# Rows set aside for instruction fetches, one bound register for all indexed transfers, and a branch laid out the other way, in an argmax, gather and scatter kernel

## The chip, the cores and the metric

The kernel runs on one core of a Trainium2 chip. The time is the device time of one execution in microseconds (us), and medians of several executions are given. All runs told here are "fast" (granted clock 1.0). The profile's span, which starts and ends inside the execution, is 1.8 us shorter than the time.

## The reference

```python
def setup_inputs():
    B, S, H = (8, 2048, 2560)
    return {'scores': randn(B, S, S), 'values': randn(B, S, H)}      # float32, seeded

def reference(scores, values):
    best_j = np.argmax(scores, axis=2)                    # a row number for each row of scores
    gathered = values[b_idx, best_j, :].copy()
    out = np.zeros_like(values)
    np.add.at(out, (b_idx, best_j, slice(None)), gathered)
    return out
```

Row j of `out` is row j of `values` times the number of times that j was an argmax in its batch. With these inputs 6,131 of the 16,384 rows have the count 0, 5,875 the count 1 and 4,378 a count of 2 or more.

## The kernel before

VectorE finds the argmaxes, TensorE counts them, and GpSimd issues indirect transfers of 128 rows: single rows straight from `values` to `out`, repeated rows in through SBUF (scaled by ScalarE) and out again, zero rows from a row of zeros. A transfer's index list names a row of `out` or a number out of bounds. In the trace a row moved is a packet of 10,240 B and 385 ns; an entry out of bounds moves no row and leaves a 4 B packet of 9 ns (medians).

```python
def scatter_rows_in_dram(nc, out, in_, idx, bound): ...   # single rows; takes its bound from a register
last_row = nc.gpsimd.to_reg(B * S - 1)
...
ZCAP, MCAP = 7, 5
ZLAST = 12
CORR = 56
...
def scatter(v, idx, note=writes_out):                     # zero rows and repeated rows
    note(nc.gpsimd.indirect_dma_start(
        out=out_flat[:, :], out_offset=bass.IndirectOffsetOnAxis(ap=idx, axis=0),
        in_=v, in_offset=None, bounds_check=B * S - 1, oob_is_err=False))
```

A transfer of 128 rows is split over 16 DMA engines, 8 rows to each: with such shares one assignment fits all 44,928 data packets of the trace (the sorting is in the prediction). In the last batch the kernel evens the engines out: it counts for each engine the rows of all other work and hands out the 746 zero rows of that batch so that the sums agree, within a cap of `CORR` rows between engines.

```python
def level_engines(rank):
    ...   # copies: single rows by engine; load: zero rows of the other batches, repeated rows of all
    nc.vector.scalar_tensor_tensor(out=work[:], in0=load[:, 1, :], scalar=2.0, in1=load[:, 0, :], op0=ALU.mult, op1=ALU.add)
    nc.vector.tensor_tensor(out=work[:], in0=work[:], in1=copies[:], op=ALU.add)
    nc.vector.tensor_reduce(out=top[:], in_=work[:], op=ALU.max, axis=X)
    ...   # more = min(top - work, CORR); even = the rest divided by 16, rounded up
    nc.vector.tensor_scalar(out=quota[:], in0=more[:], scalar1=even[:, 0:1], scalar2=None, op0=ALU.add)
    ...   # the zero rows are dealt out in the order of the engines until they are used up
```

At the end comes code for inputs that overflow the kernel's fixed numbers of transfers. It isn't needed here, and a branch passes it by; then GpSimd waits for the last transfers.

```python
more = nc.values_load(over_i[0:1, 0:1], engines=[ET.Pool, ET.DVE, ET.PE], min_val=0, max_val=2)
with tc.If(more > 0):
    ...   # one transfer at a time, long
last = nc.gpsimd.wait_ge(landed, 16 * n_free[0])
```

Of the kernel before, what the change touches and what calls it, by code (L numbers as in the profile page):

```python
# [8 lines left out]
FP32 = mybir.dt.float32  # L9
# [4 lines left out]
ALU = mybir.AluOpType  # L14
P = 128
# [21 lines left out]
def kernel(  # L37
# [6 lines left out]
    nc = tc.nc  # L44
    B, S, S2 = scores.shape
# [11 lines left out]
    NE = 16  # L57
    LE = P // NE
    ZCAP, MCAP = 7, 5
    ZLAST = 12  # L60
    ZHEAD = 4
    CORR = 56

    values_flat = values.rearrange("b s h -> (b s) h")
    out_flat = out.rearrange("b s h -> (b s) h")
    last_row = nc.gpsimd.to_reg(B * S - 1)

    consts = ctx.enter_context(tc.tile_pool(name="consts", bufs=1))
# [41 lines left out]
    nc.vector.tensor_scalar(out=rowset[:], in0=lane_f[:, 0:NE], scalar1=part8_f[:, 0:1], scalar2=None, op0=ALU.is_equal)  # L110
    up_f = consts.tile([P, NE], FP32)
    nc.vector.tensor_scalar(out=up_f[:], in0=lane_f[:, 0:NE], scalar1=-1.0, scalar2=NE - 1.0, op0=ALU.mult, op1=ALU.add)
    tots = consts.tile([P, 2, B], FP32)
    most = consts.tile([P, 1], FP32)
    notone = consts.tile([P, NT], FP32)
# [22 lines left out]
    while x < B * NT:  # L138
        n = 1
# [12 lines left out]
    def writes_out(ins):  # L152

        tc.declare_no_dep(ins.ins, group="out", reason="disjoint rows")
        tc.add_to_no_dep_group("out", ins.ins)

    def after_waits(ins):
        tc.declare_no_dep(ins.ins, group="zrow", reason="GpSimd has waited for the transfers ahead of it")
# [12 lines left out]
    def gather(v, idx, note=lambda ins: None):  # L171
        note(nc.gpsimd.indirect_dma_start(  # L172
            out=v, out_offset=None, in_=values_flat[:, :],
            in_offset=bass.IndirectOffsetOnAxis(ap=idx, axis=0), bounds_check=B * S - 1, oob_is_err=False))

    def scatter(v, idx, note=writes_out):
        note(nc.gpsimd.indirect_dma_start(  # L177
            out=out_flat[:, :], out_offset=bass.IndirectOffsetOnAxis(ap=idx, axis=0),
            in_=v, in_offset=None, bounds_check=B * S - 1, oob_is_err=False))

    vslot = [0]
    tiles = [0]
# [6 lines left out]
    def find_maxima(rows, t, am):  # L189

        g = t % G
        if g == 0:
            am = small.tile([P, G, 8], U32, name="am")
        mx = small.tile([P, 8], FP32, name="mx")
        nc.vector.max(out=mx[:], in_=rows)  # L195
        nc.vector.max_index(out=am[:, g, :], in_max=mx[:], in_values=rows)  # L196
        return am
# [60 lines left out]
    def level_engines(rank):  # L258
# [12 lines left out]
            out=share[:], in0=tots[:].rearrange("p c b -> p (c b)").unsqueeze(1).to_broadcast([P, NE, 2 * B]),  # L271
            in1=up_f[:].unsqueeze(2).to_broadcast([P, NE, 2 * B]), op=ALU.add)
# [3 lines left out]
        nc.vector.tensor_reduce(out=load[:, 1, :], in_=share[:, :, B:2 * B], op=ALU.add, axis=X)  # L276
        work = lev.tile([P, NE], FP32)
        nc.vector.scalar_tensor_tensor(out=work[:], in0=load[:, 1, :], scalar=2.0, in1=load[:, 0, :], op0=ALU.mult, op1=ALU.add)
        nc.vector.tensor_tensor(out=work[:], in0=work[:], in1=copies[:], op=ALU.add)
        top = lev.tile([P, 1], FP32)  # L280
        nc.vector.tensor_reduce(out=top[:], in_=work[:], op=ALU.max, axis=X)
        more = lev.tile([P, NE], FP32)
# [3 lines left out]
        fits = lev.tile([P, 1], FP32)  # L286
        nc.vector.tensor_single_scalar(out=fits[:], in_=zeros, scalar=float(NE * (NT * LE - CORR)), op=ALU.is_le)
        nc.vector.tensor_scalar(out=more[:], in0=more[:], scalar1=float(CORR), scalar2=fits[:, 0:1], op0=ALU.min, op1=ALU.mult)
        all_more = lev.tile([P, 1], FP32)
# [14 lines left out]
            out=past[:], in0=rank.unsqueeze(2).to_broadcast([P, NT, NE]),  # L304
            in1=ends[:].unsqueeze(1).to_broadcast([P, NT, NE]), op=ALU.is_ge)
# [13 lines left out]
    def value_steps(b, cnt_ps):  # L319
# [43 lines left out]
        if b == B - 1:  # L363
            level_engines(rank[:, 0, :])
# [42 lines left out]
        def gathers():  # L407
            for k in range(MCAP):
                v = stage()
                gather(v, mi[:, k:k + 1])  # L410
                nc.scalar.activation(out=v, in_=v, func=mybir.ActivationFunctionType.Copy, bias=0.0,  # L411
                                     scale=mc[:, k:k + 1])
                staged.append(v)
                if rest:
                    copy_once(rest.pop(0))

        def zeros(columns):
            for k in columns:
                scatter(zrow[:], zi[:, k:k + 1], free_running)
                if rest:  # L420
                    copy_once(rest.pop(0))
# [3 lines left out]
        if b == 0:  # L425
            zeros(range(ZHEAD))

# [3 lines left out]
            yield  # L431
            zeros(range(ZHEAD, nz))
        else:
            gathers()
            zeros(range(ZHEAD))
        for k in range(MCAP):

            scatter(staged[k], mi[:, k:k + 1], writes_out if b * MCAP + k < B * MCAP - NV else free_running)
        if b > 0:
            zeros(range(ZHEAD, nz))  # L440
        assert not rest
# [39 lines left out]

    more = nc.values_load(over_i[0:1, 0:1], engines=[ET.Pool, ET.DVE, ET.PE], min_val=0, max_val=2)
    spilt = tc.alloc_semaphore("spilt")
    with tc.If(more > 0):

        n_spilt = 0
        last = nc.gpsimd.wait_ge(landed, 16 * n_free[0])

        def one_by_one(ins):
            nonlocal n_spilt, last  # L490
            writes_out(ins)
            after_waits(ins)
            tc.add_to_no_dep_group("zrow", ins.ins)
            ins.then_inc(spilt, 16)
            tc.info.no_tile_sem_insts.add(ins.ins.name)
            n_spilt += 1
            with tc.issue_after(ins.ins):
                last = nc.gpsimd.wait_ge(spilt, 16 * n_spilt)

        for b in range(B):  # L500
            for k in range(ZLAST if b == B - 1 else ZCAP, NT):
                with tc.issue_after(last.ins):
                    scatter(zrow[:], zero_i[:, b * NT + k:b * NT + k + 1], one_by_one)

        for b in range(B):
            for k in range(MCAP, NM):
                i = b * NM + k
                with tc.issue_after(last.ins):
                    gather(zrow[:], many_i[:, i:i + 1], one_by_one)
                with tc.issue_after(last.ins):  # L510
                    scaled = nc.gpsimd.tensor_scalar(
                        out=zrow[:], in0=zrow[:], scalar1=many_c[:, i:i + 1], scalar2=None, op0=ALU.mult)
                after_waits(scaled)
                with tc.issue_after(scaled.ins):
                    scatter(zrow[:], many_i[:, i:i + 1], one_by_one)

        for b in range(FAST):
            cnt_ps = psum_c.tile([P, NT], FP32)
            am = None
            for t in range(NT):  # L520
                rows = room[:, 0:S]
                with tc.issue_after(last.ins):
                    after_waits(nc.gpsimd.dma_start(out=rows, in_=scores[b, t * P:(t + 1) * P, :]))
                am = find_maxima(rows, t, am)
                if t % G == G - 1:
                    count_places(am, t, cnt_ps)
            cnt = fin.tile([P, NT], FP32)
            nc.vector.tensor_copy(cnt[:], cnt_ps[:])
            some_f = fin.tile([P, NT], FP32)
            nc.vector.tensor_scalar(out=some_f[:], in0=cnt[:], scalar1=0.0, scalar2=BIG, op0=ALU.is_equal, op1=ALU.mult)  # L530
            nc.vector.scalar_tensor_tensor(out=some_f[:], in0=some_f[:], scalar=float(b * S), in1=row_f[:], op0=ALU.add, op1=ALU.add)
            nc.vector.tensor_copy(some_i[:, b * NT:(b + 1) * NT], some_f[:])
            for t in range(NT):
                with tc.issue_after(last.ins):
                    empty = nc.gpsimd.memset(zrow[:], 0.0)
                after_waits(empty)
                with tc.issue_after(empty.ins):
                    gather(zrow[:], some_i[:, b * NT + t:b * NT + t + 1], one_by_one)
                with tc.issue_after(last.ins):
                    scaled = nc.gpsimd.tensor_scalar(out=zrow[:], in0=zrow[:], scalar1=cnt[:, t:t + 1], scalar2=None, op0=ALU.mult)  # L540
                after_waits(scaled)
                with tc.issue_after(scaled.ins):
                    one_by_one(nc.gpsimd.dma_start(out=out_flat[b * S + t * P:b * S + (t + 1) * P, :], in_=zrow[:]))
# [34 lines left out]
```

## Time and profile before

| | before |
|---|---|
| time, median of 6 | 826.94 us (826.55 to 827.45) |
| span of the profile | 825.1 us |
| DMA engines | 347.13 MB, mean 421 GB/s, full in 39 of 40 slices |
| VectorE, GpSimd busy | 73%, 33% |
| GpSimd's last transfer issued | 809.97 us |
| instruction fetches (queues 14 and 8) | 17 of 8192 B and 6 of 16,384 B |

The prediction reads the busy rows and the queues line by line. What it tells of windows is this view of the kernel before; columns are the window, its length, busy time and instructions of each engine, TensorE's clock, the mean busy share of the 16 DMA engines, and GB/s.

```profile
814.00:816.00 2.00, 0.00 (x0) 0.00 (x0) 0.00 (x0) 0.00 (x0) 0.00 (x0) 1.00 0.96 389
816.00:818.00 2.00, 0.00 (x0) 0.00 (x0) 0.00 (x0) 0.00 (x0) 0.00 (x0) 1.00 0.65 226
818.00:820.00 2.00, 0.00 (x0) 0.00 (x0) 0.00 (x0) 0.00 (x0) 0.00 (x0) 1.00 0.26 87
820.00:822.00 2.00, 0.00 (x0) 0.00 (x0) 0.00 (x0) 0.00 (x0) 0.00 (x0) 1.00 0.10 31
```

Read the last two figures of each line. No compute engine works any more. The 0.10 of the last line is a tenth of 16 engines: one or two engines at work while the others have nothing left.

### The profile page before, as it was taken

How to read it: one execution, taken by the hardware profiler on the slowest of the kernel's cores; microseconds unless marked ns; L12 is line 12 of the kernel's file. 1: busy time of each engine (PE TensorE's matmuls, PEld its weight loads, DVE VectorE, ACT ScalarE, POOL GpSimd, SP SyncE). 2: the span in 40 equal slices, each digit the busy share in tenths (PEclk: the TensorE clock that was granted, in tenths of full speed). 3: DMA queues.
4: the chain of work that ended last, by engine and by line, in shares of the span. 5: the costliest groups of instructions: out<-in, count | busy, mean ns of one | idle time of the engine just before them, and what ended most of it. 6: DMA issues, size and time to landing. Idle time of an engine off the chain costs nothing.

```text
span 825.1 us, 3112 instructions
## 1 busy us (share of the span) xinstructions
PE 31.8 (4%) x786; PEld 29.2 (4%) x786; DVE 599.9 (73%) x733; ACT 168.2 (20%) x107; POOL 271.8 (33%) x277
## 2 busy tenths in 40 slices
PE   0211210000000000000000000000000000000000
PEld 0111110000000000000000000000000000000000
DVE  5886879999999999999999999999998000000000
ACT  6664730041012100023000032000410320230230
POOL 0027241011232505201513111515166266346342
DMA  9999999999999999999999999999999999999996
GB/s 383 427 436 428 432 415 416 439 421 426 421 425 428 429 429 432 430 429 428 429 420 419 428 428 431 438 420 418 426 427 421 423 425 422 424 422 424 424 427 260
DMA packets 44951, 347.13 MB, mean 421 GB/s; under 512 B 18662, under 2 KB 18662, under 8 KB 18662
## 3 DMA queue, kind: packets, MB, share of 16 engines
q0 software_dynamic: 38736, 212.67, 62.0%
q1 hardware_dynamic: 6192, 134.22, 37.9%
q14 instruction: 17, 0.14, 0.1%
q8 instruction: 6, 0.10, 0.0%
HBM read 354.42 MB, written 300.15 MB: 793 GB/s over the span
## 4 chain that ended last, share of the span: by engine, by line
DMA 30%; DVE 26%; issue 21%; POOL 11%; another core or an unknown queue 6%; ACT 2%; PE 0%; POOLq 0%; SPq 0%; ACTq 0%; DVEq 0%
DMA room<-in_values_dram,many_i 23%; DVE am L196 9%; DVE mx L195 9%; POOL out_dram L33 6%; DVE mx L219 4%; DMA out_dram<-room,many_i 4%; POOL out_dram L177 4%; DMA room<-in_scores_dram 4%; ACT less L222 2%; POOL room L172 2%; DVE oh L372 1%; DVE oh_lo L205 1%; PE cnt_ps L232 0%; SPq L241 0%
## 5 line engine op out<-in xcount | busy, mean ns | idle before, releaser
L196 DVE FIND_INDEX8 am<-mx,room 128x8 uint32<-128x2048 f32 x96 | 219.3, 2285 | 0.0
L195 DVE MAX8 mx<-room 128x8 f32<-128x2048 f32 x96 | 218.8, 2279 | 0.0
L411 ACT ACTIVATE room<-room,many_c 128x2560 f32<-128x2560 f32 x40 | 96.7, 2426 | 587.1 <-DMA room<-in_values_dram,many_i 587.0
L33 POOL DMA_INDIRECT out_dram<-in_values_dram,ones_i x128 | 130.8, 1022 | 106.4 <-DVE m L343 68.0
L177 POOL DMA_INDIRECT out_dram<-room,many_i x40 | 38.9, 973 | 259.4 <-ACT room L411 256.3
L172 POOL DMA_INDIRECT room<-in_values_dram,many_i x40 | 41.1, 1027 | 152.9 <-DMA out_dram<-room,many_i 134.9
L219 DVE MAX8 mx<-room 128x8 f32<-128x2048 f32 x32 | 72.8, 2286 | 11.7 <-DMA room<-in_scores_dram 11.7
L222 ACT ACTIVATE less<-room,mx 128x2048 bf16<-128x2048 f32 x32 | 64.0, 2001 | 38.7 <-DVE sole L229 17.5
L177 POOL DMA_INDIRECT out_dram<-zrow,zero_i x61 | 59.9, 983 | 18.8 <-issue 18.8
L213 PE MATMUL cnt_ps<-oh_hi,oh_lo 128*128 128x16 bf16 x96 | 6.1, 174 | 417.5 <-DVE oh_hi L209 398.2
L213 PEld LDWEIGHTS <-oh_lo 128*128 128x128 bf16 x96 | 6.3, 105 | 417.4 <-DVE oh_lo L205 397.3
L232 PEld LDWEIGHTS <-less 128*128 128x128 bf16 x512 | 16.1, 104 | 83.0 <-ACT less L222 60.8
L372 DVE TENSOR_TENSOR oh<-lo,fill_f 128x2048 f16<-128x2048 uint32 x8 | 18.3, 2292 | 0.3
L232 PE MATMUL cnt_ps<-sole,less 128*128 128x1 bf16 x512 | 18.2, 165 | 0.0
L205 DVE TENSOR_TENSOR oh_lo<-lo,lane_f 128x512 bf16<-128x512 uint32 x24 | 16.6, 692 | 0.3
L229 DVE TENSOR_SCALAR sole<-n_less 128x1 bf16<-128x1 f32 x32 | 4.8, 150 | 15.0 <-ACT less L222 14.7
L196 DVE MATCH_VALUE_LOAD am<-mx,room 128x8 f32 x96 | 8.8, 92 | 3.3
L230 PE MATMUL cnt_ps<-sole,minus 128*128 128x16 bf16 x32 | 5.5, 171 | 83.1 <-DVE sole L229 81.4
L390 PE MATMUL l_ps<-put,oh 128*128 128x32 f16 x128 | 4.7, 188 | 71.1 <-DVE put L387 71.1
L390 PEld LDWEIGHTS <-oh 128*128 128x128 f16 x128 | 4.7, 104 | 72.3 <-DVE oh L372 61.9
L222 ACT ACTIVATION_READ_ACCUMULATOR less<-room,mx 128x1 f32 x32 | 6.0, 187 | 0.0
L201 DVE TENSOR_SCALAR lo<-am 128x4 uint32<-128x4 uint32 x24 | 4.9, 203 | 0.8
(101 smaller groups left out, 80.1 us busy)
## 6 DMA issues: line engine op xcount, KB each, us to landing
room<-in_scores_dram SPq DMA_DIRECT2D x24, 4096.0 KB, 17.4
room<-in_scores_dram SPq DMA_DIRECT2D x9, 2048.0 KB, 23.9
room<-in_scores_dram SPq DMA_DIRECT2D x8, 1024.0 KB, 8.8
room<-in_scores_dram SPq DMA_DIRECT2D x2, 3072.0 KB, 14.2
out_dram<-in_values_dram,ones_i POOLq DMA_INDIRECT x128
out_dram<-zrow,zero_i POOLq DMA_INDIRECT x61
room<-in_values_dram,many_i POOLq DMA_INDIRECT x40, 32.5
out_dram<-room,many_i POOLq DMA_INDIRECT x40, 45.2
```

The source lines that it names most:

```text
L33: return eng.add_instruction(ins)
L172: note(nc.gpsimd.indirect_dma_start(out=v, out_offset=None, in_=values_flat[:, :], in_offset=bass.IndirectOffsetOnAxis(ap=idx, axis=0), bo ...
L177: note(nc.gpsimd.indirect_dma_start(out=out_flat[:, :], out_offset=bass.IndirectOffsetOnAxis(ap=idx, axis=0), in_=v, in_offset=None, bound ...
L195: nc.vector.max(out=mx[:], in_=rows)
L196: nc.vector.max_index(out=am[:, g, :], in_max=mx[:], in_values=rows)
L205: nc.vector.tensor_tensor(out=oh_lo[:], in0=lo[:].unsqueeze(2).to_broadcast([P, G, P]), in1=lane_f[:].unsqueeze(1).to_broadcast([P, G, P]) ...
L213: nc.tensor.matmul(out=cnt_ps[:], lhsT=oh_lo[:, k, :], rhs=oh_hi[:, k, :], start=(t == G - 1 and k == 0), stop=(t == NT - 1 and k == G - 1))
L219: nc.vector.max(out=mx[:], in_=rows)
L222: nc.scalar.activation(out=less[:], in_=rows, func=mybir.ActivationFunctionType.Sign, bias=mx[:, 0:1], scale=-1.0, accum_out=n_less[:])
L232: nc.tensor.matmul(out=cnt_ps[:, c:c + 1], lhsT=less[:, c * P:(c + 1) * P], rhs=w, start=False, stop=(t == NT - 1 and c == NT - 1))
L372: nc.vector.tensor_tensor(out=oh[:], in0=lo[:].unsqueeze(2).to_broadcast([P, NT, P]), in1=fill_f[:].unsqueeze(1).to_broadcast([P, NT, P]), ...
L411: nc.scalar.activation(out=v, in_=v, func=mybir.ActivationFunctionType.Copy, bias=0.0, scale=mc[:, k:k + 1])
```

## The change

The intent: the levelling should count the time that two DMA engines spend on instruction fetches, as 5 and 12 rows' worth of work (`FETCH`), so that they get fewer zero rows; GpSimd should load the bound B*S-1 into a register once and not for each transfer; and the usual way through the branch should be the one without a jump.

```diff
+    FETCH = {2: 5, 3: 12}
...
+    fetch = consts.tile([P, NE], FP32)
+    nc.vector.memset(fetch[:], 0.0)
+    for e, n in FETCH.items():
+        nc.vector.memset(fetch[:, e:e + 1], float(n))
...  # in gather and in scatter
-            ..., bounds_check=B * S - 1, oob_is_err=False))
+            ..., bounds_check=last_row, oob_is_err=False))
...  # in level_engines, behind the line that makes work
+        nc.vector.tensor_tensor(out=work[:], in0=work[:], in1=fetch[:], op=ALU.add)
...
-    with tc.If(more > 0):
+    with tc.If(more > 0, preferred_fallthrough_block=False):
```

More of the change, by code (lines that the diff above doesn't have):

```diff
@@ L173, in gather @@
             out=v, out_offset=None, in_=values_flat[:, :],
-            in_offset=bass.IndirectOffsetOnAxis(ap=idx, axis=0), bounds_check=B * S - 1, oob_is_err=False))
+            in_offset=bass.IndirectOffsetOnAxis(ap=idx, axis=0), bounds_check=last_row, oob_is_err=False))
     def scatter(v, idx, note=writes_out):
@@ L178, in scatter @@
             out=out_flat[:, :], out_offset=bass.IndirectOffsetOnAxis(ap=idx, axis=0),
-            in_=v, in_offset=None, bounds_check=B * S - 1, oob_is_err=False))
+            in_=v, in_offset=None, bounds_check=last_row, oob_is_err=False))
     vslot = [0]
```

## The prediction

> **What bounds the kernel now.** I read four views in this order: the page's busy rows, the DMA rows of the page, the timeline and the waits around the end, and the DMA rows of the last 25 us alone.
>
> The page's busy rows come first.
>
> ```profile
> DVE  5886879999999999999999999999998000000000
> ...
> POOL 0027241011232505201513111515166266346342
> DMA  9999999999999999999999999999999999999996
> GB/s 383 427 436 428 432 415 416 439 421 426 421 425 428 429 429 432 430 429 428 429 420 419 428 428 431 438 420 418 426 427 421 423 425 422 424 422 424 424 427 260
> ```
>
> Each digit is one fortieth of 825.1 us. VectorE has nothing to do after slice 31, GpSimd is never full, and the DMA engines are at 9 in every slice but the last. So it is the data that sets the time, 347 MB at 421 GB/s, and a wait or an instruction saved on any engine is worth nothing unless it takes work off the DMA engines or evens it out over them. Only the 6 at the end is open.
>
> The page's queue rows tell what else those engines carry.
>
> ```profile
> q0 software_dynamic: 38736, 212.67, 62.0%
> q1 hardware_dynamic: 6192, 134.22, 37.9%
> q14 instruction: 17, 0.14, 0.1%
> q8 instruction: 6, 0.10, 0.0%
> ```
>
> There are 23 instruction fetches. On the average of 16 engines that is 0.1%; on the one engine that takes a fetch it is time in full.
>
> The end of the timeline shows GpSimd's last transfers; columns are start, duration, instruction, idle time before it.
>
> ```profile
> 805.18 0.96 POOL L177 DMA_INDIRECT out_dram<-zrow,zero_i  x1 [0.30 <-issue]
> ...
> 809.00 0.97 POOL L177 DMA_INDIRECT out_dram<-zrow,zero_i  x1 [0.30 <-issue]
> ```
>
> GpSimd has issued everything at 809.97. The 15.1 us that follow are the DMA engines emptying their rings, then the closing barrier. The same view of 800 to 826, for the DMA engines, in forty slices of 0.65 us:
>
> ```profile
> DMA  9899999999979979999998998763221100000000
> ...
> q14 instruction: 4, 0.03, 0.3%
> ```
>
> The share falls from 8 to 0 over slices 24 to 32, some 5 us, and a remainder under half a tenth runs on to 822.5: the engines do not end together. In two-us windows it is 0.96 (814 to 816), 0.65, 0.26, 0.10 (820 to 822), 0.03. Summing what each window from 810 to 822.5 lacks gives 4.7 us: the end would come 4.7 us sooner if the same packets were spread perfectly.
>
> **Which engine is last, and why.** The profile doesn't number the engines, but its packet records can be sorted by engine: a packet starts 4 ns before the previous one on its engine ends, a row moved (10,240 B) takes 385 ns and a row skipped 9 ns, and which rows of a transfer are moved follows from counting each argmax in the reference's seeded inputs. I counted these, put each transfer's 128 rows in 16 shares, and one assignment fits all 44,928 data packets with the counted rows on every engine. All rows: 6,131 zero, 4,378 repeated (moved twice), 5,875 single, which is 20,762, the number of 10,240 B packets recorded. Times of the records are 10.51 us above span times; I give span times.
>
> The counted rows by the kernel's own levelling: 1299 on thirteen engines, 1298 on engine 9, 1293 on 12, 1284 on 15. (The quotas add up to 761 for 746 rows, so the last engine comes short by 15; engine 12 wanted more than CORR's 56.) Ends: engine 3 at 822.54, 9 at 820.66, 4 at 820.33, 2 at 819.64; the eleven others with 1299 rows, 4 among them, have a mean of 817.44 and a standard deviation of 1.20; engine 15 ends at 811.6. So engine 3 alone sets the end. It carries seven of the 17 queue-14 fetches, engine 2 six, engine 1 two, engine 4 one (one lies after the end). Engine 3's cost 2.18 us themselves and 2.36 us more on the packets right behind them, 4.54 us or 11.9 rows of 0.381 us: the 12 rows that the change sets aside. Engine 2's cost 3.79 us, 9.9 rows; the change sets 5 aside. The six 16 KB fetches fall on six different engines.
>
> [...] 8192 B packets of q14 stand between data packets, 309 ns each when undisturbed. [...] The trace shows 8192 B for q14 and 16,384 B for q8; and GpSimd's compare-and-branch at 801.85 is followed by its next instruction only at 807.16, with a q14 fetch on engine 2 at 805.5 and another at 810.2.
>
> **The change, part by part.**
> 1. *Rows set aside.* I repeat the levelling's integer arithmetic with 12 and 5 added to engines 3 and 2. Zero rows of the last batch move: engine 3 has 1289 rows instead of 1299, engine 2 1296, engine 9 1288 and 12 1283 (both now cut by CORR), 15 has 1295; the eleven others have 1301. In time, engine 3: 822.54 - 10 x 0.381 = 818.7. Engine 9: 820.66 - 3.8 = 816.9. Engine 2 about 818.5. The eleven: + 2 x 0.381 = + 0.76, mean 818.2. The end is now the latest of these eleven. If each keeps its delays, that is engine 4 at 820.33 + 0.76 = 821.1, 1.4 us before the old end. If the delays are drawn anew, the latest of eleven lies some 1.6 deviations over the mean, 818.2 + 1.9 = 820.1, 2.4 us before it. If engine 4's delay was a freak, the next is engine 11 at 818.33 + 0.76 = 819.1, 3.4 us before.
> 2. *The branch.* Not taken, GpSimd, VectorE and TensorE go straight on. For GpSimd that saves the two fetches on engine 2 after 801.85 (309 + 164 and 309 + 194 ns, 0.98 us) and some 5 us of waiting, but its next job is to wait until 823.55 for the last transfers: nothing on the path, only a further margin for engine 2. VectorE's fetch at 644.3 on engine 3 (309 ns) may go as well.
> 3. *The shared register.* Of 269 indirect transfers 141 lose their own register move. It lay in the sequencer beside work: L177 (with a move) and L33 (without) both show 0.30 us of idle before them, so the pitch stays about 1.27 us. [...] Zero on the path.
> 4. *Added.* Three VectorE memsets of 0.06 to 0.07 us in the setup, where it waits 4.46 us for the first rows; one 128x16 addition of 0.17 us in the levelling, beside full DMA rings (share 1.02 there). Zero.
>
> Between the last packet (822.54) and the end of the span (825.1) lie 2.6 us of landing, wait and barrier, which stay.
>
> Sum: 827.04 less 1.4 to 3.4, central 2.3: 824.7 us.
>
> **The rivals.**
> *Another engine takes engine 3's place.* Partly counted already. Delays other than fetches, 0.3 to 0.9 us at a time on random packets, add up to between 1.2 and 6.2 us on an engine, and levelling can't see them. For it speaks engine 4, late by 2.9 us with only one fetch; against it that all ten of its companions end within 1.6 us of the mean. Were it wholly true the gain is 1.0 to 1.4 us: 825.8.
> *Over-correction.* The fetches were measured with the branch taken; with fewer of them, engines 2 and 3 merely end early. Engines 9 and 12 come short by 13 and 18 rows because of CORR; all 16 shares add up to the same 20,762 rows, so this costs the others 37/16 = 2.3 rows, 0.9 us, which is in the 1301. If VectorE still makes seven fetches, engine 3 ends with the others. No loss: 824.7.
> *The clearing of GpSimd's branch and moves matters by itself.* If GpSimd were the bound, 141 moves and 5 us would come to several us, below 822. The DMA share of 1.01 to 1.02 in every window from 600 to 810 says that the rings are never empty; against it, and worth nothing.
> *Nothing, or worse.* If the engine numbers behind the fetches moved from load to load, the rows set aside would sit on wrong engines: engine 3's place is taken by some engine with 1301 rows and seven fetches, 0.8 us later than now: 827.8. The queues' engines are the same through the whole trace (engine 3's fetches come from 53.6 to 644 us), so I hold this unlikely.
>
> **Range and chances.** The three cases of part 1 give 825.6, 824.7 and 823.6; the three runs of before spread over 0.7 us. Eight in ten: 823.2 to 826.3. Two per cent is 16.5 us; even perfect spreading is worth 4.7, so faster by over 2% 0.01, slower 0.01, the same 0.98.
>
> **What would show it.** The DMA rows of the last 25 us should fall to nothing without the thin remainder, the last packet near 820.2 rather than 822.5. Engine 3's last row near 818.5, the last engine one of those with 1301 rows. Two or three fewer q14 packets, and no gap of 5 us after GpSimd's branch. L33's and L177's pitch still near 1.27 us. The prediction is wrong if engine 3 or 2 is still last, if the last engine's extra delay is over 3 us again, if the span after the last packet grows beyond 2.6 us, or if the time falls below 823, which would mean that GpSimd's issue mattered after all.

Cut from it, and marked, are statements that no trace of this case shows: how an engine serves its queues, which partition belongs to which engine, what a taken branch fetches, and how many bytes an instruction takes. No term of the sum went with them: 827.04 us less 1.4 to 3.4, central 2.3, came to 824.7 us, from counted rows, packet times and the engines' ends. Part 2's view that the new layout spares two fetches and 5 us of waiting, and the fetch that part 3's moves were to spare (not in the sum), and the "two or three fewer q14 packets" with them, are estimates.

## The result, and the profile after

The changed kernel takes 825.18 us (median of 6, 824.76 to 825.83) against 826.94 us, 1.76 us less. The ratio is 0.9979, 95% interval 0.9966 to 0.9992. A ratio is the mean time of one kernel's fast runs over the mean of the other's in the same rounds, so it isn't quite the ratio of the medians quoted. The prediction was 824.7 us within 823.2 to 826.3, the same within 2%.

The changed kernel's page, DMA rows and queues:

```profile
DMA  9999999999999999999999999999999999999997
...
q8 instruction: 6, 0.10, 0.0%
q14 instruction: 15, 0.12, 0.0%
```

The last digit went from 6 to 7, and there are 15 q14 packets for 17. The windows of the end in the changed kernel, to be held against those of before:

```profile
814.00:816.00 2.00, 0.00 (x0) 0.00 (x0) 0.00 (x0) 0.00 (x0) 0.00 (x0) 1.00 0.94 369
816.00:818.00 2.00, 0.00 (x0) 0.00 (x0) 0.00 (x0) 0.00 (x0) 0.00 (x0) 1.00 0.76 277
818.00:820.00 2.00, 0.00 (x0) 0.00 (x0) 0.00 (x0) 0.00 (x0) 0.00 (x0) 1.00 0.21 52
820.00:822.00 2.00, 0.00 (x0) 0.00 (x0) 0.00 (x0) 0.00 (x0) 0.00 (x0) 1.00 0.05 15
```

From 816 to 818 the engines are busier (0.76 for 0.65), from 818 on less: the fall is steeper. But 0.05 of 16 engines still runs from 820 to 822: 0.8 of one engine. There is still one straggler.

Which one, the packets tell. I sorted the packets of the changed kernel by engine as the prediction does for the one before, and again each engine has the rows that the levelling's arithmetic gives it. "Foretold" is the end before plus 0.381 us for each row more or less.

| DMA engine | rows before | end before, us | rows after | foretold | end after, us |
|---|---|---|---|---|---|
| 3 | 1299 | **822.54** | 1289 | 818.7 | 818.91 |
| 9 | 1298 | 820.66 | 1288 | 816.9 | 817.46 |
| 4 | 1299 | 820.32 | 1301 | 821.1 | **821.62** |
| 2 | 1299 | 819.64 | 1296 | 818.5 | 818.30 |
| 12 | 1293 | 818.31 | 1283 | 814.5 | 814.67 |
| 15 | 1284 | 811.55 | 1295 | 815.7 | 814.52 |
| mean of the eleven others with 1299, 1301 (4 among them) | | 817.44 | | 818.2 | 818.32 |

Engine 3 came back into the crowd, and engine 4, third from last before, is the last. The end of the data moved by 0.92 us, not by the 3.6 us that engine 3 gained.

The two profiled executions differ by 1.15 us in span (825.11 and 823.96). That splits so: the last data packet 0.92 us earlier; GpSimd's wait ended 1.01 us after that packet before and 1.14 us after it now; and from the end of the wait to the end of the span it took 1.55 us before and 1.21 us now. The last of these is a gain of 0.34 us that the prediction did not have.

GpSimd's side of the end, in the chain of waits of the kernel before, columns start, duration, what (POOLq is GpSimd's sequencer; L484 is the branch, L482 the loading of its condition):

```profile
800.91 0.88 POOLq L482
...
806.45 0.73 POOL out_dram L177
...
807.28 0.02 POOLq L484
```

and of the changed kernel, where the branch is L490 and the loading L488:

```profile
801.05 0.10 POOLq L490
...
801.18 0.04 POOLq L490
...
806.82 0.03 POOLq L488
```

Before, GpSimd's sequencer ran on behind the branch at 807.2 only. Now it does the work behind the branch at once, up to 801.2 — and then stands still until 806.6 all the same. The trace has a second compare-and-branch there, at 801.18 of the span, and no instruction of the overflow's lines behind it: the jump over that code was moved, not removed. The instruction itself took 53 ns before and 40 and 41 ns now, but the next one on GpSimd came 5.3 us after the branch before (801.85 to 807.16) and 5.4 us after the second one now (801.18 to 806.58), with the DMA share at 1.02 to 1.03; the first one now (799.15) was followed after 0.09 us. In all fourteen profiles that gap is 5.1 to 5.5 us. And the pitch of the transfers in the timeline of the changed kernel, with all 141 moves (29 ns each before) gone:

```profile
807.81 0.96 POOL L182 DMA_INDIRECT out_dram<-zrow,zero_i  x1 [0.30 <-issue]
809.08 0.96 POOL L182 DMA_INDIRECT out_dram<-zrow,zero_i  x1 [0.30 <-issue]
```

1.27 us from start to start with 0.30 us of idle, as before.

### The profile page after: what moved, and what is told of

Its sections match the earlier page's. It is cut to its first block, busy times and chain, and to the rows that moved or that the text cites. A ratio compares the mean times of both kernels' runs of the same rounds, so it can differ in the third digit from the quotient of the medians.

```text
span 824.0 us, 2978 instructions
## 1 busy us (share of the span) xinstructions
PE 31.8 (4%) x786; PEld 29.1 (4%) x786; DVE 600.3 (73%) x737; ACT 168.1 (20%) x107; POOL 271.3 (33%) x277
## 4 chain that ended last, share of the span: by engine, by line
DMA 35%; DVE 27%; another core or an unknown queue 23%; ACT 5%; POOL 5%; issue 4%; PE 0%; SPq 0%; ACTq 0%; POOLq 0%; DVEq 0%
DMA room<-in_values_dram,many_i 23%; DVE am L201 9%; DVE mx L200 9%; DMA out_dram<-room,many_i 8%; DVE mx L224 5%; ACT room L417 4%; DMA room<-in_scores_dram 4%; POOL out_dram L33 3%; ACT less L227 2%; POOL out_dram L182 2%; POOL room L177 1%; DVE oh L378 1%; DVE oh_lo L210 1%; DVE sole L234 0%
## 5 line engine op out<-in xcount | busy, mean ns | idle before, releaser
L234 DVE TENSOR_SCALAR sole<-n_less 128x1 bf16<-128x1 f32 x32 | 4.8, 149 | 14.9 <-ACT less L227 14.7
## 6 DMA issues: line engine op xcount, KB each, us to landing
room<-in_scores_dram SPq DMA_DIRECT2D x2, 3072.0 KB, 13.9
```

## The experiments

Theory: the end is set by the DMA engine that finishes last; fetches, and delays that belong to an engine, add to its rows; the change takes engine 3 out of last place, and engine 4 then holds the end. Rivals: GpSimd's moves and branch bring the gain; or the delays are drawn anew each time, so that engine 4 was last by chance. Twelve runs of ten kernels were made (the change itself ran again, two of its versions ran twice), all with correct results and five timed executions each. All lie within 2% of the kernel before. What is told here is smaller than that, and the 95% intervals say how far it can be trusted. Runs of one batch of four share a chip and the runs of the kernel before; "last packet" is from each kernel's one profile.

| run | median, us | before, same chip | ratio (95%) | last data packet, us (engine) |
|---|---|---|---|---|
| level_only | 825.55 | 827.15 | 0.9979 (0.9965 to 0.9993) | 821.83 (4) |
| no_level | 826.30 | 827.15 | 0.9990 (0.9976 to 1.0004) | 821.84 (3) |
| four | 824.43 | 827.15 | 0.9969 (0.9955 to 0.9982) | 820.25 (7) |
| all_delays | 825.49 | 827.15 | 0.9975 (0.9962 to 0.9989) | 821.12 (7) |
| more_before | 829.67 | 826.88 | 1.0036 (1.0023 to 1.0050) | 825.11 (3) |
| more_after | 826.24 | 826.88 | 0.9996 (0.9982 to 1.0009) | 821.85 (3), 821.84 (4) |
| wrong_engines | 826.65 | 826.88 | 0.9998 (0.9984 to 1.0011) | 823.44 (3) |
| three_only | 824.89 | 826.88 | 0.9981 (0.9967 to 0.9994) | 820.36 (4) |
| whole | 824.67 | 826.20 | 0.9981 (0.9967 to 0.9994) | 821.40 (7) |
| no_level_again | 825.85 | 826.20 | 0.9997 (0.9983 to 1.0011) | 821.83 (3) |
| four_again | 823.52 | 826.20 | 0.9973 (0.9960 to 0.9987) | 819.19 (8) |
| refined | 823.66 | 826.20 | 0.9973 (0.9959 to 0.9986) | 818.53 (11) |

The kernel before itself differs by 0.95 us between the chips of the batches, so times of different batches are compared by their ratios.

### The parts by themselves

**level_only**: the changed kernel with the other two parts undone.

```diff
-            ..., bounds_check=last_row, oob_is_err=False))
+            ..., bounds_check=B * S - 1, oob_is_err=False))
-    with tc.If(more > 0, preferred_fallthrough_block=False):
+    with tc.If(more > 0):
```

> The levelling with its rows set aside, without the shared register and without the new branch. Theory: the gain is all in the levelling, so this is as fast as the whole change: 825.2 us, 1.8 us under the kernel before, engine 4 last again at about 821.6 us of the span. Rival, that GpSimd's moves and branch are worth time by themselves: half of the gain or less, 826 us or more.

It has the whole change's ratio (0.9979 both), and engine 4 is last at 821.83 us. The levelling alone accounts for the gain as far as the timing can tell.

**no_level** and **no_level_again**: the changed kernel with the rows set aside left at zero.

```diff
-    for e, n in FETCH.items():
-        nc.vector.memset(fetch[:, e:e + 1], float(n))
```

> The shared register and the branch, with the array of set-aside rows left at zero. Theory: engine 3 is last as in the kernel before, at 822.5 us of the span, and the time is 826.9 us, within 0.4 of the kernel before. Rival (moves and branch): 825.2 to 826.0 us.

The first run came out 0.85 us under the kernel before, between the theory and the rival, with an interval that takes in 1. So it was run again.

> The register and the branch without rows set aside, again, since its first run came out 0.8 us under the kernel before with an interval that takes in no difference. Theory, that the 0.8 us were chance in engine 3's delay: 826.5 to 827.2 us. Rival, that the register or the branch takes time off engine 3: 826.3 us or less again, with engine 3's last packet near 821.8 us as in the first run, and an interval that leaves out 1.

The second difference is 0.35 us, and the interval takes in 1 again; the 826.3 of the expectation was meant for a kernel before at 827.15, and here that one takes 826.20, so the ratio decides. Engine 3 is last in both, at 821.8 us, 0.7 us sooner than in the profile of before; in wrong_engines below, with the same register and branch, it is last at 823.44 with one row more. That speaks against the register and the branch as the cause of those 0.7 us, but weakly, since it is one profile and of the slowest of its five executions, 0.8 us over their median. What does come with register and branch shows in all fourteen profiles: from the end of GpSimd's wait to the end of the span it takes 1.55 us in the three that have neither (before, level_only, more_before) and 1.21 us in the eleven that have both. The difference sits in one place, from the start of GpSimd's closing drain to its next instruction, 0.43 against 0.10 us. So register and branch together shorten the close by 0.34 us. It is likely the branch, which lays out the code there, but no run has one without the other, so that isn't shown. In the medians the two together are worth no more than timing can part from zero.

### Whether fetches take the time of their engine

**more_before** and **more_after**: 512 instructions more on VectorE after its last work, in the kernel before and in the changed one.

```diff
         nc.vector.tensor_reduce(out=over_i[:], in_=over[:], op=ALU.max, axis=mybir.AxisListType.X)
+        idle = fin.tile([P, 1], FP32)
+        for _ in range(512):
+            nc.vector.memset(idle[:], 0.0)
```

> The kernel before with 512 more memsets of one column on VectorE after its last work, when it is idle (some 30 us beside full DMA rings). [...] that is four more fetches on engine 3, the last engine. Theory, that a fetch costs engine 3 some 0.65 us (0.31 itself, 0.34 on the packet behind it): engine 3 ends 2.6 us later, time 829.5 us. Rival, that engine 3 is slow for a reason of its own and the fetches cost what their bytes cost, 0.31 us: 828.2 us. Rival, that fetches lie beside the data: 826.9 us.

The four fetches were an estimate.

The page of more_before, its row of queue 14 (17 in the kernel before):

```profile
q14 instruction: 21, 0.17, 0.0%
```

Four fetches more for 512 instructions, one for each 128 in this run, and all four on engine 3 in the sorted packets. Engine 3's last packet went from 822.54 to 825.11, 2.57 us later, where 2.6 was expected. The median is 2.79 us over the kernel before. Both rivals fail: 0.3 us per fetch would be 1.2 us, and no cost 0. One pair of profiles alone would be thin, since engine 3's end varies by 0.7 us with the same rows (822.54 before, 821.83 in no_level_again). But the packets say the same: behind the fetches at 667.6, 704.7 and 715.1 us the next row took 739 to 756 ns instead of 385, which makes 0.66 to 0.68 us with the fetch's own 309 ns. Engine 9 ended later too, at 824.00 us for 820.66, though no fetch was added to it; of that below.

> The same 512 memsets in the changed kernel, where engine 3 ends at 818.9 us of the span, 2.7 us before the last engine, 4. Theory: engine 3 goes to 821.5 us and engine 4 stays last at 821.6, so the time stays at 825.2 to 825.6 us. Rival, that the added instructions cost time on VectorE or GpSimd: 2 us or more over the changed kernel.

Here too four fetches were added (19 for 15). Engine 3 went from 818.91 to 821.85 and stands beside engine 4 at 821.84: the fetches that cost the kernel before 2.8 us fell into the 2.7 us of room that engine 3 had. But the time, 826.24 us, is 0.6 us over the expectation and its ratio (0.9996) 0.0015 over that of the whole change, 1.2 us. Part of it may be that the last of two equals comes later than the last of one. And engines 8, 9, 11 and 12, which the added instructions should have left alone, ended 1.4 to 3.7 us later than in the kernel before (more_before) and 2.7 to 3.3 us later than in the changed kernel (more_after). The packets show where much of that was lost. Between 726 and 760 us, after the last memset and with no fetch on any engine, engine 9 lost 5.3 us in more_before, engine 8 3.0, engine 12 2.9 and engine 11 0.7, in pauses and in rows that took longer than 385 ns; the others kept their pitch. The stretch is slow without memsets too: engine 9 lost 1.5 to 3.5 us in it in each of the twelve profiles without them, engine 12 up to 1.1, the others that could be followed 0.2 at most. What stops these engines there stays open.

### Whether the rows must be on these engines

**wrong_engines**:

```diff
-    FETCH = {2: 5, 3: 12}
+    FETCH = {11: 5, 10: 12}
```

> The changed kernel with the 12 and the 5 rows set aside on engines 10 and 11 instead of 3 and 2. Theory: engine 3 with 1300 rows is last at 822.9 us of the span, time 827.3 us, 0.4 over the kernel before. Rival, that any shift of the last rows gains: 825.2 us.

Engine 3 is last, at 823.44 us with 1300 rows (822.9 was expected). The median is 0.2 us under the kernel before, not 0.4 over it, and the interval holds both; the profile is of the slowest of the five executions. The rival's 825.2 is far off: this other shift of rows gains nothing that can be told from zero.

**three_only**:

```diff
-    FETCH = {2: 5, 3: 12}
+    FETCH = {3: 12}
```

> The changed kernel with 12 rows on engine 3 and none on engine 2. Theory: engine 2 ends at 820.3 us of the span, still before engine 4 at 821.6, so the 5 rows of engine 2 are worth nothing yet and the time is that of the changed kernel, 825.2 us. Rival, that engine 2's rows carry part of the gain: 826 us.

The ratio is that of the whole change. Engine 2, without its 5 rows, ends at 819.9 us, before engine 4. The 5 rows of engine 2 are worth nothing while engine 4 ends later.

### Whether engine 4's delay comes back

**four** and **four_again**:

```diff
-    FETCH = {2: 5, 3: 12}
+    FETCH = {2: 5, 3: 12, 4: 8}
```

> The changed kernel with 8 more rows set aside, on engine 4, the one that ends last in it. Rows by the levelling's arithmetic: engine 4 has 1294 for 1301, most others 1302 for 1301. Theory, that an engine's delay belongs to the engine and comes back in every run: engine 4 ends at 819 us rather than 821.6, the last engine (3, 10 or 11) at 819.4 to 820.2, time 823.0 to 823.8 us. Rival, that the delays are drawn anew in every run: the last of the others is as likely to lie at 821 to 822, time 824.8 to 825.6 us, no gain on average.

Engine 4 ends at 817.7 us, and the last is engine 7 at 820.25. The time is 2.7 us under the kernel before, where the change itself had 1.8, and 0.6 us over what was expected.

**whole** and **four_again**, on one chip:

> The whole change again, beside three others on one chip. Theory: engine 4 is last at 821.6 to 821.9 us of the span, time 825.2 to 825.6 us, a ratio to the kernel before of 0.998. Rival, that engine 4 was last by chance in the runs so far: another engine is last and the time differs by more than 0.5 us from 825.4.

In this profile engine 7 is last at 821.40 and engine 4 next, at 820.58: the rival is right for one profile of the changed kernel, not for the other. The time by its ratio is where it was.

> The changed kernel with 8 rows on engine 4 as well, again, to stand beside the whole change on one chip. Theory: some 1.0 us under the whole change, 824.2 to 824.6 us, with an engine other than 4 last. Rival, that its first result was a difference of chips: within 0.4 us of the whole change.

823.52 against 824.67 us: 1.15 us under the whole change on the same chip. The two intervals overlap, but in the first batch four and level_only lie nearly as far apart (0.9969 and 0.9979). This version is faster than the kernel before, both times clear of the interval; that it is faster than the changed kernel as well is likely, since it came out so twice, but not shown.

Engine 4's delay is a lasting one. Taking 0.381 us per row off each engine's end in the eight fully sorted or matched profiles without memsets (before, after, level_only, no_level, four, all_delays, wrong_engines, three_only) leaves its delay. In rows, counted from the engine that is least delayed on the average of these profiles (so that an early one can be below zero), median and range:

| engine | median | range | fetches on it |
|---|---|---|---|
| 3 | 16.9 | 14.9 to 18.5 | 7 of 8192 B |
| 9 | 14.5 | 12.1 to 15.9 | 1 of 16,384 B |
| 12 | 12.2 | 11.6 to 13.9 | 1 of 16,384 B |
| 4 | 11.0 | 9.0 to 12.9 | 1 of 8192 B |
| 2 | 8.7 | 7.8 to 12.2 | 5 or 6 of 8192 B |
| 7 | 6.3 | -0.9 to 10.9 | none |

Engines 4, 9 and 12 are late by 3.4 to 6.1 us every time, with one fetch each. In the changed kernel engines 9 and 12 don't show because the cap gives them 13 and 18 rows too few, about what they need. Engine 7 is of the other kind: now early, now late by 4 us. Engine 15 is among the early ones (-0.3 to 4.9 rows).

### How far this can be taken

**all_delays**:

```diff
-    FETCH = {2: 5, 3: 12}
-    CORR = 56
+    FETCH = {0: 1, 1: 2, 2: 8, 3: 16, 4: 11, 5: 2, 6: 4, 9: 13, 10: 4, 11: 5, 12: 11, 14: 2, 15: 1}
+    CORR = 72
```

> The changed kernel with rows set aside on every engine in the measure of the delay it showed on the average of the two profiles (16 rows on engine 3, 13 on 9, 11 on 4 and 12, 8 on 2, 5 and less on the others), and the cap on the correction raised from 56 to 72 rows so that engines 9 and 12 get theirs. Theory, delays belong to engines: all engines but 15 end within a microsecond, the last at 818.2 to 819.0 us of the span, time 821.8 to 822.7 us. Rival, delays drawn anew: the spread of ends stays at 1.2 to 1.5 us and the last engine lies at 820 or later, 823.7 us or more.

A miss: 825.49 us where 821.8 to 822.7 was expected. In its profile fourteen engines end between 816.9 and 818.8 us, as the theory has it, but engine 5 at 820.4 and engine 7 at 821.12: two draws of the part of the delay that does not stay. My reading, which no run tests by itself: by moving rows onto the engines that had been early in two profiles, the version took away their room for such a draw.

**refined**: the same with rows chosen on eight profiles, so that engine 7 gets 6 and engine 5 gets 5 set aside.

> Rows set aside for all engines, chosen on the delays that eight profiles showed for each engine (16 rows on engine 3, 12 on 9, 11 on 12, 10 on 4, 9 on 2, 6 and less on the others), cap 72. Theory, that a delay has a part that stays with the engine and a part drawn anew (0.3 to 1.3 us of deviation by engine): putting those delays on these rows gives a last engine at 819.0 us on the average, time some 823 us, at best; with fresh draws 823.4 to 824.4 us, and never under 822.5. Rival, that nothing is left to gain over the version with engine 4 alone because the drawn part sets the end: 824.2 us or more.

Its profile has the earliest last packet of all. Its end, the windows of the same view:

```profile
814.00:816.00 2.00, 0.00 (x0) 0.00 (x0) 0.00 (x0) 0.00 (x0) 0.00 (x0) 1.00 0.96 374
816.00:818.00 2.00, 0.00 (x0) 0.00 (x0) 0.00 (x0) 0.00 (x0) 0.00 (x0) 1.00 0.54 170
818.00:820.00 2.00, 0.00 (x0) 0.00 (x0) 0.00 (x0) 0.00 (x0) 0.00 (x0) 1.00 0.02 0
820.00:822.00 2.00, 0.00 (x0) 0.00 (x0) 0.00 (x0) 0.00 (x0) 0.00 (x0) 1.00 0.00 0
```

From 0.54 to 0.02 within one window: this is what level engines look like. That execution took 822.26 us, but the five spread from there to 824.42, and the median of 823.66 is as good as that of four_again beside it (823.52, ratio 0.9973 both). The median lies within the 823.4 to 824.4 that the theory gave for fresh draws, and the best execution under its "never under 822.5"; both numbers were meant for a kernel before that takes some 0.7 us more than on this chip. In substance the rival holds: over the version with engine 4 alone no gain shows. That the part drawn anew now sets the end fits with this, but one profile doesn't show it.

## Why the prediction was right, and where it wasn't

**What bounds the kernel**, the DMA engines and at the end the last of them: right. level_only and no_level show that the levelling carries the gain, and more_before shows that fetches move the end by moving engine 3.

**Part 1, the rows set aside**: right in its rows, and near in its ends. Engine 3 ended 0.2 us from where it was foretold, the mean of the eleven 0.1 us. Of its three cases, engine 4 keeping its delay was nearest to the profile (821.1 foretold, 821.62 measured), and I gave it too little weight: the central 824.7 us leaned on delays drawn anew. One of the prediction's own signs of being wrong came true with it, "if the last engine's extra delay is over 3 us again": engine 4 ended 3.3 us over the mean of the eleven. Two of its checks failed as well: the last packet came at 821.6, not near 820.2, and the thin remainder stayed (0.05 of 16 engines). The runs show a lasting part (engine 4: 9.0 to 12.9 rows) and a drawn part (engine 7). The measured 825.18 lies between the first case's 825.6 and the centre, 0.5 us from it. Part of that closeness is luck: the centre took 2.3 us for the levelling, where level_only measured 1.6, and left out the 0.34 us of part 2.

**Part 2, the branch**: the step that failed, though it is small. It was an estimate, with no trace behind it. "GpSimd, VectorE and TensorE go straight on. For GpSimd that saves the two fetches on engine 2 after 801.85": they are still there, at 804.9 and 809.6 us of the changed kernel's span, and so is a gap of 5.4 us, now behind a second branch that jumps over the unused code. And "nothing on the path" is wrong by 0.34 us: the closing part, which was to stay at 2.6 us, is shorter by that in each kernel with the new branch and the register. VectorE's fetch on engine 3 didn't go either; it has seven before and after.

**Part 3, the register**: right as far as it can be told. The pitch stayed at 1.27 us. Of the two q14 packets that are gone, one lay after the end, at 825.0 us; the other was engine 2's, which has six in the three kernels with the moves and five in the sorted ones without. It is one of those long before the branch (engine 2 had three before 700 us, now two), which speaks for the moves, but no run undid the register alone.

**Part 4, the added instructions**: nothing in the profile speaks of a cost. The memsets (0.06 to 0.07 us each) ran at 1.0 to 1.2 us of the changed kernel's span, where VectorE had its first rows only at 5.53, and the addition (0.17 us) at 627.5, where the DMA share is 1.02 (620 to 636).

**The rivals.** "Another engine takes engine 3's place" is what happened, by 0.92 us between the two profiles and 1.76 in the medians, against "1.0 to 1.4". "Over-correction" cost what it was said to cost and no more. "GpSimd's branch and moves matter by themselves" holds for the 0.34 us at the close, and no more of it can be told from zero. "Nothing, or worse" fell: the fetches of VectorE were on engine 3 in each fully sorted profile but for one early packet, which no_level's sorting puts on engine 7, before the rows' patterns tell engines apart.

What stays open: why engines 4, 9 and 12 are late by nearly the same time in every run with hardly a fetch on them. Part of it can be placed: 1.5 to 3.5 us of engine 9's delay fall between 726 and 760 us, and 0.65 to 0.76 us of engine 4's after 776 us, where its one fetch lies; the rest of engine 4's came before 690 us. Open too is why the extra instructions on VectorE delayed engines that fetch nothing for it, and whether the branch or the register shortens the close.

## What to carry to other kernels

Here the DMA engines were full in 39 of 40 slices, and the span ended 2.6 us after the last engine's last packet (822.54 of 825.1 us). In such a kernel sort the packets by engine before levelling anything, and look at who is second: taking engine 3 out of the way by 3.6 us moved the last packet by 0.92 us only, the distance to engine 4's new end. A fetch of instructions cost its engine twice its own packet here (0.64 us for 0.31), and VectorE's fetches fell on one engine (all four of more_before on engine 3). Level by delays that come back in several profiles (engine 4: 9.0 to 12.9 rows), and leave the engines whose delay changes from run to run some room (engine 7: -0.9 to 10.9).
